# Differential attention: the low-half product of the scores on 64 of the 128 rows, in two row halves

## The chip, the cores and the metric

The program runs on one core of one Trainium2 chip. The metric is device microseconds of one execution; it was run three times, and the median is quoted. One further execution was recorded by the profiler, and all rows below are of that one.

## The reference

Two layers of a hybrid backbone over 128 context tokens and 1024 latent tokens. The change lies in the differential attention of the odd layer (4 heads; per head two softmaxes `p` = 0, 1 with 64 dimensions each; 1152 keys: 128 cached context keys and 1024 own ones):

```
s = einsum('bhqpd,bhkpd->bhpqk', qi, keys) * DH_C ** -0.5
p = softmax(s, axis=-1)
w = p[:, :, 0] - lam * p[:, :, 1]
o = einsum('bhqk,bhkv->bhqv', w, vals)
```

The context tokens have an attention of their own over 128 keys, through the same helper functions.

## The kernel before

Products that need more than the multiplier's one-pass precision are made from high and low halves: a value x is split into hi (rounded) and lo = x - hi, both of type fp32r, and `mm3` (lines 205 to 207) adds hi·hi, lo·hi and hi·lo in PSUM. The general matrix products of the projections and the feed-forward parts go through it.

`attention` (line 1300 on) does the 1024 latent queries of four heads, in 32 steps `n`, eight tiles of 128 queries per head. For each head `load` (L1348 to L1363) brings from DRAM: `q`, on 128 partitions the 64 dimensions of the queries' high halves and below them the 64 of the low halves, for both softmaxes; `kh`, the keys' high halves, twice (partitions 0 to 63 and 64 to 127); `kl`, their low halves, also twice; and the values `v`. One matmul of `q` with `kh` thus contracts 128 rows and gives (q hi + q lo)·k hi, and one with `kl` gives (q hi + q lo)·k lo.

- `tails` (L1308): for two tiles and both softmaxes, four products of 128 queries with the last 128 keys in one PSUM bank, each `kh` then `kl`; one copy to SBUF (`xt`, ScalarE) and one maximum for all four (`xm`, L1318, VectorE).
- `weights` (L1321): for each softmax the scores of the first 1024 keys (`s`, two PSUM banks, two such tiles in all), per bank `kh` then `kl` (L1328), four matmuls of 128 by 512; then `softmax` (L1199): maximum over `s` on VectorE (L1205), combined with `xm` (L1207), the exponentials on ScalarE (L1214) with their sums, the sums added (L1216), the reciprocal (L1217).
- `weigh` (L1220) calls `softmax` twice and merges the two results (L1227, L1228).
- `values` (L1334): nine transposes of the merged weights in three PSUM banks of tag `b` (L1340), three copies to `w` (ScalarE, VectorE, ScalarE), and nine full-precision matmuls with `v` (L1344), which the trace records as 18.

TensorE is filled between these steps by the output projection of finished parts (`mix_group`, tiles `w` and `ad`, L205 to L207) and, at the beginning, by the modulation of the second layer (`ada`, L384), whose weights `adaw` are 1 MB per transfer.

The order of the instructions on each engine is set when the program is built: a scheduler places each instruction by its priority and by a simulated timeline (`urgent` raises the priority), and the engines then run that fixed order. TensorE, VectorE and ScalarE each work through their own list, and an instruction that waits holds what stands behind it. All of the loads named here are issued by SyncE.

Of the kernel before, what the change touches and what calls it, by code (L numbers as in the profile page):

```python
# [10 lines left out]
F32 = mybir.dt.float32  # L11
F32R = mybir.dt.float32r
U32 = mybir.dt.uint32
AF = mybir.ActivationFunctionType
ALU = mybir.AluOpType
# [3 lines left out]
P = 128  # L19
# [3 lines left out]
NTOK = 1152  # L23
# [171 lines left out]
class Kern:  # L195
# [1000 lines left out]
                self.attention_prompt(al, "p", (2 * hb, 2 * hb + 1))  # L1196


    def softmax(self, pool, parts, tag, r, bufs=2):  # L1199

        nc = self.nc
        n = sum(x.shape[1] for x, _ in parts)
        p = pool.tile([P, n], F32, tag=f"{tag}{n}", name=tag, bufs=bufs)
        mx = pool.tile([P, 1], F32, tag=f"smx{n}", name="smx")
        nc.vector.tensor_reduce(mx, parts[0][0], AX.X, ALU.max)  # L1205
        if len(parts) == 2:
            nc.vector.tensor_scalar(mx, mx, parts[1][1], -0.125, ALU.max, ALU.mult)  # L1207
        else:
            nc.vector.tensor_scalar(mx, mx, -0.125, None, ALU.mult)
        sm = pool.tile([P, 2], F32, tag=f"ssm{n}", name="ssm", bufs=4)  # L1210
        o = n
        for i, (x, _) in reversed(list(enumerate(parts))):
            o -= x.shape[1]
            nc.scalar.activation(p[:, o:o + x.shape[1]], x, AF.Exp, scale=0.125, bias=mx, accum_out=sm[:, i:i + 1])  # L1214
        if len(parts) == 2:
            nc.vector.tensor_tensor(sm[:, 0:1], sm[:, 0:1], sm[:, 1:2], ALU.add)  # L1216
        nc.vector.reciprocal(r, sm[:, 0:1])  # L1217
        return p, sm[:, 0:1]

    def weigh(self, pool, scores, r1, tag, bufs=2):  # L1220

        nc = self.nc
        r2 = pool.tile([P, 1], F32, tag="r2" + tag, name="r2")
        with self.urgent():
            p1, s1 = self.softmax(pool, scores(0), "p0", r1, bufs)
            p2, _ = self.softmax(pool, scores(1), "p1", r2)
        nc.vector.tensor_scalar(r2, r2, self.nlam, s1, ALU.mult, ALU.mult)  # L1227
        nc.vector.scalar_tensor_tensor(p1, p2, r2, p1, ALU.mult, ALU.add)  # L1228
        return p1

    def attn_tokens(self, ps, r1, ob, ss, junk):
# [71 lines left out]
    def attention(self, hp, pool, last):  # L1303


        nc = self.nc

        def tails(t, q, kh, kl):  # L1308

            ps = self.bank("b")  # L1310
            for j in range(4):
                for x, kx in enumerate((kh, kl)):
                    nc.tensor.matmul(ps[:, 128 * j:128 * j + 128], q[:, j % 2, 128 * (t + j // 2):128 * (t + j // 2) + 128],
                                     kx[:, j % 2, 1024:1152], start=(x == 0), stop=(x == 1))
            xt = pool.tile([P, 4, P], F32, tag="xt", name="xt", bufs=3)
            self.copy(nc.scalar, xt, ps.rearrange("p (j k) -> p j k", j=4))
            xm = pool.tile([P, 4], F32, tag="xm", name="xm", bufs=3)
            nc.vector.tensor_reduce(xm, xt, AX.X, ALU.max)  # L1318
            return [(xt[:, j], xm[:, j:j + 1]) for j in range(4)]

        def weights(t, q, kh, kl, tail):  # L1321
            r1 = pool.tile([P, 1], F32, tag="r1", name="r1", bufs=4)

            def scores(p):
                s = self.ps["s"].tile([P, 1024], F32, tag="s", name="s", bufs=self.psb["s"] // 2)
                for k0 in (0, 512):
                    for x, kx in enumerate((kh, kl)):
                        nc.tensor.matmul(s[:, k0:k0 + 512], q[:, p, 128 * t:128 * t + 128], kx[:, p, k0:k0 + 512],  # L1328
                                         start=(x == 0), stop=(x == 1))
                return [(s, None), tail[2 * (t % 2) + p]]  # L1330

            return self.weigh(pool, scores, r1, "s", 3), r1

        def values(p1, r1, v, ob, ss):  # L1334
            w = pool.tile([P, NT, P], F32, tag="w", name="w", bufs=2)
            for g in range(3):
                pt = self.bank("b", 384)
                for j in range(3):
                    c = 3 * g + j
                    nc.tensor.transpose(pt[:, 128 * j:128 * j + 128], p1[:, 128 * c:128 * c + 128], self.ident)  # L1340
                self.copy((nc.scalar, nc.vector, nc.scalar)[g], w[:, 3 * g:3 * g + 3], pt.rearrange("p (c t) -> p c t", c=3))
            po = self.bank("b", P)
            for c in range(NT):
                nc.tensor.matmul(po, w[:, c], v[:, c], start=(c == 0), stop=(c == NT - 1))  # L1344
            junk = pool.tile([P, P], F32, tag="junk", name="junk")
            self.attn_tokens(po, r1, ob, ss, junk)

        def load(h, after=None):  # L1348

            q = hp.tile([P, 2, 1024], F32R, tag="q", name="q")  # L1350
            kh = hp.tile([P, 2, NTOK], F32R, tag="kh", name="kh")
            kl = hp.tile([P, 2, NTOK], F32R, tag="kl", name="kl")
            v = hp.tile([P, NT, P], F32, tag="v", name="v")
            if after is not None:
                for x in (q, kh, kl, v):
                    self.copy(nc.vector, x[:, 1, 0:1], after)
            nc.sync.dma_start(q[:].bitcast(F32), self.qT[2 * h:2 * h + 2].rearrange("j p t -> p j t"))
            for x in range(2):
                nc.sync.dma_start(kh[64 * x:64 * x + 64].bitcast(F32), self.kT[2 * h:2 * h + 2, 0:64].rearrange("j p t -> p j t"))
                nc.sync.dma_start(kl[64 * x:64 * x + 64].bitcast(F32), self.kT[2 * h:2 * h + 2, 64:128].rearrange("j p t -> p j t"))  # L1360
            nc.sync.dma_start(v[:, 0], self.A["cache_diff_v"][0, 0, h])
            nc.sync.dma_start(v[:, 1:], self.vals[1:, :, 128 * h:128 * h + 128].rearrange("i p d -> p i d"))
            return (q, kh, kl), v  # L1363

        loaded, tail, before, done = {}, {}, None, None
        for n in range(33):
            h, t = n // 8, n % 8
            if n == 0:
                loaded[0] = load(0)
                tail[0] = tails(0, *loaded[0][0])  # L1370
            if n < 32:
                if t == 0:
                    ob = pool.tile([P, 8, P], F32, tag="ob", name="ob")
                    ss = pool.tile([P, 8], F32, tag="ss", name="ss")
                w = weights(t, *loaded[h][0], tail[n // 2])
                now = w + (loaded[h][1], ob[:, t], ss[:, t:t + 1])
                if t == 2 and h < 3:
                    loaded[h + 1] = load(h + 1, w[1] if h == 0 else None)
                if t % 2 and n < 31:
                    tail[n // 2 + 1] = tails((t + 1) % 8, *loaded[(n + 1) // 8][0])  # L1380
            if n:
                values(*before)
                if n in (8, 16, 24, 28, 32):
                    a = slice(0, 8) if n < 28 else slice(0, 4) if n < 32 else slice(4, 8)
                    done = n, old[0][:, a], old[2], 128 + 128 * a.start, last if n > 24 else None
                    self.attn_norm(pool, done[1], old[1][:, a])
            if done and n in (done[0] + 2, 32):
                self.attn_out("b", *done[1:])
                done = None
            before, old = now, (ob, ss, h)  # L1390
            yield
# [243 lines left out]
```

## Time and profile before

| what | us |
|---|---|
| median of 3 runs | 3513.89 (3511.16 to 3518.72) |
| profiled execution, its own time | 3512.49 |
| span of that execution | 3510.7 |
| TensorE busy in the span | 3329.9 (95%) |
| VectorE, ScalarE, GpSimd busy | 1880.7, 1349.7, 870.9 |

The share of an engine is an average over stages with different limits, and a matmul's busy time contains the tail in which its results drain. What a change in one stage is worth is read from that stage, which here lies between 2272 us (first `tails`) and 2605 us (last `values`) of the span.

### The profile page before, as it was taken

Reading aid. Unit: us, or ns where it says so; the run is one execution under the profiler, and the core shown is the slowest. Engines: PE = TensorE matmul, PEld = TensorE weight load, DVE = VectorE, ACT = ScalarE, POOL = GpSimd, SP = SyncE. Lnnn points to the kernel's source line nnn. Section 1 sums busy time; section 2 is a strip of 40 time slices with the busy share of each in tenths; the row PEclk is TensorE's granted clock in tenths of the full one; section 3 lists DMA queues with packets and bytes.
Section 4 is the critical chain, followed back from the end, with each engine's and each line's share of the span. In section 5 each row is a group of like instructions: output and inputs, shape, how many; then the busy total and the mean of one; then the engine's idle time right before and its main releaser. Section 6 shows DMA issues by size and latency. Waiting matters only on the chain.

```text
span 3510.7 us, 55883 instructions
## 1 busy us (share of the span) xinstructions
PE 3329.9 (95%) x23022; PEld 3023.3 (86%) x23022; DVE 1880.7 (54%) x3342; ACT 1349.7 (38%) x2412; POOL 870.9 (25%) x596
## 2 busy tenths in 40 slices
PE   5999999888899999999999999989988999999998
PEld 2999999756689999999988999857767999999997
DVE  5658987488652333333372446458886233343334
ACT  5334333454543222232264434356565322232223
POOL 2432230001442222232240003301124222232214
PEclk7999999999899999999999999999998999999999
DMA  6445434483511110111143342583123111111104
GB/s 218 137 148 151 119 103 137 162 293 121 169 60 49 37 42 28 52 49 43 36 148 114 114 141 75 159 265 97 39 97 103 43 43 30 43 54 43 38 29 138
DMA packets 272700, 348.08 MB, mean 99 GB/s; under 512 B 14354, under 2 KB 231597, under 8 KB 266302
## 3 DMA queue, kind: packets, MB, share of 16 engines
q1 hardware_dynamic: 269294, 334.82, 30.2%
q0 software_dynamic: 3152, 9.70, 0.9%
q8 instruction: 181, 2.97, 0.4%
q14 instruction: 73, 0.60, 0.1%
HBM read 266.58 MB, written 77.89 MB: 98 GB/s over the span
## 4 chain that ended last, share of the span: by engine, by line
PE 78%; DVE 8%; DMA 6%; ACT 3%; issue 2%; POOL 2%; SPq 1%; POOLq 0%; DVEq 0%; ACTq 0%
PE g L206 9%; PE g L207 8%; PE g L205 8%; PE a L206 7%; PE a L205 7%; PE a L207 7%; PE d L205 5%; PE d L206 5%; PE d L207 5%; DMA adaw<-in_ada_w 2%; PE b L1344 1%; DVE f L442 1%; PE s L1328 1%; DVE acc L1002 1%; PE w L205 1%
## 5 line engine op out<-in xcount | busy, mean ns | idle before, releaser
L206 PE MATMUL g<-hTl,whi 128*128 128x388 f32 (+2 forms) x1728 | 591.1, 342 | 2.2 <-POOL hTl L218 2.2
L205 PE MATMUL g<-hTh,whi 128*128 128x388 f32 (+2 forms) x1728 | 590.6, 342 | 2.3 <-ACT hTh L445 2.3
L207 PE MATMUL g<-hTh,wlo 128*128 128x388 f32 (+2 forms) x1728 | 589.3, 342 | 0.0
L205 PE MATMUL a<-hTh,whi 128*128 128x388 f32 (+2 forms) x1248 | 427.3, 342 | 2.5 <-ACT hTh L445 1.4
L206 PE MATMUL a<-hTl,whi 128*128 128x388 f32 (+2 forms) x1248 | 427.3, 342 | 2.4 <-POOL hTl L218 2.3
L207 PE MATMUL a<-hTh,wlo 128*128 128x388 f32 (+2 forms) x1248 | 423.8, 342 | 0.1
L1002 DVE TENSOR_TENSOR acc<-d,acc 128x512 f32<-128x512 f32 x288 | 197.6, 688 | 334.0 <-PE d L207 332.7
L1104 POOL TENSOR_TENSOR ta<-ta,tg 128x386 f32<-128x386 f32 x132 | 135.7, 1028 | 916.6 <-ACT tg L1103 882.4
L205 PEld LDWEIGHTS g<-hTh,whi 128*128 128x128 f32 x1728 | 328.2, 190 | 6.7 <-ACT hTh L445 2.9
L206 PEld LDWEIGHTS g<-hTl,whi 128*128 128x128 f32 x1728 | 327.7, 190 | 6.6 <-POOL hTl L218 2.9
L207 PEld LDWEIGHTS g<-hTh,wlo 128*128 128x128 f32 x1728 | 327.5, 190 | 2.0
L205 PE MATMUL d<-dh,ah 128*128 128x512 f32 x792 | 312.7, 395 | 1.3 <-DVE acc L1002 1.3
L206 PE MATMUL d<-dl,ah 128*128 128x512 f32 x792 | 312.1, 394 | 0.0
L207 PE MATMUL d<-dh,al 128*128 128x512 f32 x792 | 312.0, 394 | 0.0
L476 ACT ACTIVATE tg<-g,cols,cols 128x386 f32<-128x386 f32 x132 | 88.8, 673 | 499.3 <-PE g L207 499.0
L218 POOL TENSOR_TENSOR wlo<-wraw,whi 128x1024 fp32r<-128x1024 f32 x90 | 217.0, 2411 | 167.7 <-ACT whi L211 167.7
L218 POOL TENSOR_TENSOR dl<-draw,dh 128x1024 fp32r<-128x1024 f32 x60 | 147.1, 2452 | 403.0 <-ACT dh L211 331.5
L205 PEld LDWEIGHTS a<-hTh,whi 128*128 128x128 f32 x1248 | 236.7, 190 | 11.3 <-issue 2.2
L206 PEld LDWEIGHTS a<-hTl,whi 128*128 128x128 f32 x1248 | 236.7, 190 | 9.6 <-POOL hTl L218 3.5
L477 DVE SCALAR_TENSOR_TENSOR tg<-g,cols,tg 128x386 f32<-128x386 f32 x132 | 81.8, 620 | 296.0 <-ACT tg L476 296.0
L207 PEld LDWEIGHTS a<-hTh,wlo 128*128 128x128 f32 x1248 | 236.6, 190 | 4.4 <-issue 1.6
L211 ACT ACTIVATE whi<-wraw 128x1024 fp32r<-128x1024 f32 x145 | 152.5, 1053 | 181.1 <-DMA wraw<-in_ffn_up 67.9
(429 smaller groups left out, 7031.8 us busy)
## 6 DMA issues: line engine op xcount, KB each, us to landing
adaw<-in_ada_w SPq DMA_DIRECT2D x48, 1024.0 KB
wraw<-in_ffn_up SPq DMA_DIRECT2D x88, 512.0 KB
draw<-in_ffn_down SPq DMA_DIRECT2D x44, 512.0 KB
wraw<-in_w_in_even SPq DMA_DIRECT2D x32, 512.0 KB
wraw<-in_w_in_odd SPq DMA_DIRECT2D x24, 512.0 KB
hgT<-po SPq DMA_DIRECT2D x16, 576.0 KB
ymid<-acc SPq DMA_DIRECT2D x18, 512.0 KB
y<-ymid SPq DMA_DIRECT2D x18, 512.0 KB
```

Source lines behind the costliest of these rows:

```text
L205: mm(out, lh, rh, start=start, stop=False)
L206: mm(out, lh, rl, start=False, stop=False)
L207: mm(out, ll, rh, start=False, stop=stop)
L211: eng.activation(out, in_, AF.Copy)
L218: eng.tensor_tensor(out, a, b, ALU.subtract)
L442: nc.vector.tensor_scalar(f[:, j], pt[:, 128 * j:128 * j + 128], mod[:, 1, g, k:k + 1], mod[:, 0, g, k:k + 1], ALU.mult, ALU.add)
L476: nc.scalar.activation(out, ps[:, 1:1 + n], AF.Identity, scale=w[1], bias=b)
L477: nc.vector.scalar_tensor_tensor(out, ps[:, 0:n], w[0], out, ALU.mult, ALU.add)
L1002: nc.vector.tensor_tensor(acc[:, i, s], ps, acc[:, i, s], ALU.add)
L1104: nc.gpsimd.tensor_tensor(ta, ta, tg, ALU.mult)
L1328: nc.tensor.matmul(s[:, k0:k0 + 512], q[:, p, 128 * t:128 * t + 128], kx[:, p, k0:k0 + 512], start=(x == 0), stop=(x == 1))
L1344: nc.tensor.matmul(po, w[:, c], v[:, c], start=(c == 0), stop=(c == NT - 1))
```

## The change

- `load` brings `kl` once: the low halves of the first softmax's keys on partitions 0 to 63, those of the second on 64 to 127. The second softmax's `q` is stored with its halves exchanged, so that the high halves of its queries lie on partitions 64 to 127. `q` takes three transfers in place of one.
- The product with `kl` contracts 64 rows, q hi with k lo, on partitions 0 to 63 for the first softmax and 64 to 127 for the second. The term q lo·k lo is no longer computed.
- `weights` writes the products of both softmaxes ahead of the first `softmax`: four with `kh`, then four with `kl`, alternating between the two.
- `tails` uses one bank and one copy per softmax, where it used one for both.
- The sums and reciprocals of both softmaxes are made by one addition and one reciprocal; one copy (`r1`) is added.
- The second of the three copies of `values` moves from VectorE to ScalarE.

```diff
     def weigh(self, pool, scores, r1, tag, bufs=2):
...
+        sm = pool.tile([P, 2, 2], F32, tag="ssm" + tag, name="ssm", bufs=4)
+        r = pool.tile([P, 2], F32, tag="r2" + tag, name="r2")
         with self.urgent():
-            p1, s1 = self.softmax(pool, scores(0), "p0", r1, bufs)
-            p2, _ = self.softmax(pool, scores(1), "p1", r2)
-        nc.vector.tensor_scalar(r2, r2, self.nlam, s1, ALU.mult, ALU.mult)
-        nc.vector.scalar_tensor_tensor(p1, p2, r2, p1, ALU.mult, ALU.add)
+            first = scores(0)
+            p1 = self.softmax(pool, first, "p0", [sm[:, i, 0:1] for i in range(2)], bufs)
+            p2 = self.softmax(pool, scores(1), "p1", [sm[:, i, 1:2] for i in range(2)])
+            if len(first) == 2:
+                nc.vector.tensor_tensor(sm[:, 0], sm[:, 0], sm[:, 1], ALU.add)
+            nc.vector.reciprocal(r, sm[:, 0])
+        nc.vector.tensor_copy(r1, r[:, 0:1])
+        nc.vector.tensor_scalar(r[:, 1:2], r[:, 1:2], self.nlam, sm[:, 0, 0:1], ALU.mult, ALU.mult)
+        nc.vector.scalar_tensor_tensor(p1, p2, r[:, 1:2], p1, ALU.mult, ALU.add)
...
         def tails(t, q, kh, kl):
-            ps = self.bank("b")
-            for j in range(4):
-                for x, kx in enumerate((kh, kl)):
-                    nc.tensor.matmul(ps[:, 128 * j:128 * j + 128], q[:, j % 2, 128 * (t + j // 2):128 * (t + j // 2) + 128],
-                                     kx[:, j % 2, 1024:1152], start=(x == 0), stop=(x == 1))
             xt = pool.tile([P, 4, P], F32, tag="xt", name="xt", bufs=3)
-            self.copy(nc.scalar, xt, ps.rearrange("p (j k) -> p j k", j=4))
+            for p in range(2):
+                ps = self.bank("b", 256)
+                x = slice(64 * p, 64 * p + 64)
+                for j in range(2):
+                    o, z = ps[:, 128 * j:128 * j + 128], slice(128 * (t + j), 128 * (t + j) + 128)
+                    nc.tensor.matmul(o, q[:, p, z], kh[:, p, 1024:1152], start=True, stop=False)
+                    nc.tensor.matmul(o, q[x, p, z], kl[x, 1024:1152], start=False, stop=True)
+                self.copy(nc.scalar, xt[:, p::2], ps.rearrange("p (j k) -> p j k", j=2))
...
         def weights(t, q, kh, kl, tail):
+            s = [self.ps["s"].tile([P, 1024], F32, tag="s", name="s", bufs=self.psb["s"] // 2) for p in range(2)]
+            z = slice(128 * t, 128 * t + 128)
+            with self.urgent():
+                for p in range(2):
+                    for k0 in (0, 512):
+                        nc.tensor.matmul(s[p][:, k0:k0 + 512], q[:, p, z], kh[:, p, k0:k0 + 512], start=True, stop=False)
+                for k0 in (0, 512):
+                    for p in range(2):
+                        x = slice(64 * p, 64 * p + 64)
+                        nc.tensor.matmul(s[p][:, k0:k0 + 512], q[x, p, z], kl[x, k0:k0 + 512], start=False, stop=True)
+
             def scores(p):
-                s = self.ps["s"].tile([P, 1024], F32, tag="s", name="s", bufs=self.psb["s"] // 2)
-                for k0 in (0, 512):
-                    for x, kx in enumerate((kh, kl)):
-                        nc.tensor.matmul(s[:, k0:k0 + 512], q[:, p, 128 * t:128 * t + 128], kx[:, p, k0:k0 + 512],
-                                         start=(x == 0), stop=(x == 1))
-                return [(s, None), tail[2 * (t % 2) + p]]
+                return [(s[p], None), tail[2 * (t % 2) + p]]
...
-                self.copy((nc.scalar, nc.vector, nc.scalar)[g], w[:, 3 * g:3 * g + 3], pt.rearrange("p (c t) -> p c t", c=3))
+                self.copy(nc.scalar, w[:, 3 * g:3 * g + 3], pt.rearrange("p (c t) -> p c t", c=3))
...
-            kl = hp.tile([P, 2, NTOK], F32R, tag="kl", name="kl")
+            kl = hp.tile([P, NTOK], F32R, tag="kl", name="kl")
...
-            nc.sync.dma_start(q[:].bitcast(F32), self.qT[2 * h:2 * h + 2].rearrange("j p t -> p j t"))
+            nc.sync.dma_start(q[:, 0].bitcast(F32), self.qT[2 * h])
+            for x in range(2):
+                nc.sync.dma_start(q[64 * x:64 * x + 64, 1].bitcast(F32), self.qT[2 * h + 1, 64 - 64 * x:128 - 64 * x])
             for x in range(2):
                 nc.sync.dma_start(kh[64 * x:64 * x + 64].bitcast(F32), self.kT[2 * h:2 * h + 2, 0:64].rearrange("j p t -> p j t"))
-                nc.sync.dma_start(kl[64 * x:64 * x + 64].bitcast(F32), self.kT[2 * h:2 * h + 2, 64:128].rearrange("j p t -> p j t"))
+                nc.sync.dma_start(kl[64 * x:64 * x + 64].bitcast(F32), self.kT[2 * h + x, 64:128])
```

The change moves instructions. In the kernel before, TensorE's list for one tile in the middle of the stage reads as follows (`s_23574` and `s_23588` are the scores of the two softmaxes of one tile, `w_...` are tiles of the output projection, `x3` stands for three in a row):

```order
L1328 MATMUL s_23574<-kh_23108,q_23107 128x512
L1328 MATMUL s_23574<-kl_23109,q_23107 128x512
L1328 MATMUL s_23574<-kh_23108,q_23107 128x512
L1328 MATMUL s_23574<-kl_23109,q_23107 128x512
L205 MATMUL w_25115<-dh_24991,mxh_24995 128x512
L206 MATMUL w_25115<-dl_24992,mxh_24995 128x512
L207 MATMUL w_25115<-dh_24991,mxl_24996 128x512
L205 MATMUL w_25115<-dh_25002,mxh_25006 128x512
L206 MATMUL w_25115<-dl_25003,mxh_25006 128x512
L207 MATMUL w_25115<-dh_25002,mxl_25007 128x512
L1328 MATMUL s_23588<-kh_23108,q_23107 128x512
L1328 MATMUL s_23588<-kl_23109,q_23107 128x512
```

Here `kh` and `kl` alternate per bank, all on 128 rows, and six matmuls of the projection lie between the two softmaxes.

In the changed kernel (L1333 is the product with `kh`, L1337 the one with `kl` on 64 rows) such a tile reads:

```order
L1333 MATMUL s_23153<-kh_22542,q_22541 128x512 x2
L1337 MATMUL s_23153<-kl_22543,q_22541 128x512 x2
L205 MATMUL w_25007<-dh_24963,mxh_24967 128x512
L206 MATMUL w_25007<-dl_24964,mxh_24967 128x512
L207 MATMUL w_25007<-dh_24963,mxl_24968 128x512
L205 MATMUL w_25007<-dh_24974,mxh_24978 128x512
L206 MATMUL w_25007<-dl_24975,mxh_24978 128x512
L207 MATMUL w_25007<-dh_24974,mxl_24979 128x512
L1333 MATMUL s_23154<-kh_22542,q_22541 128x512 x2
L1337 MATMUL s_23154<-kl_22543,q_22541 128x512 x2
L1350 MATMUL b_23121<-ident_76,p0_23006 128x128 x3
```

The written order of four and four stands only in the first tile (L1333 four times, then L1337 four times, its writes alternating between `s_22404` and `s_22405`). In the other 31 tiles the scheduler has parted the two softmaxes: two products with `kh`, two on 64 rows into the same `s` tile, so of the same row half, and then something else.

For the last keys TensorE's list in the changed kernel has (L1318 the product with `kh`, L1319 the one on 64 rows):

```order
L1318 MATMUL b_23030<-kh_22542,q_22541 128x128
L1319 MATMUL b_23030<-kl_22543,q_22541 128x128
L1318 MATMUL b_23030<-kh_22542,q_22541 128x128
L1319 MATMUL b_23030<-kl_22543,q_22541 128x128
L1350 MATMUL b_23039<-ident_76,p0_22942 128x128 x3
```

Here each product on 64 rows stands alone between two on 128 rows, as all 64 of them do. Counted over the list, the matmuls on 64 rows stand in 127 uninterrupted runs: 64 runs of one (L1319), 62 of two and one of four (L1337). Of these, 29 (16 and 13) stand ahead of the last `ada` matmul (L384), and 98 behind it.

## Rows read from the trace of the kernel before

**Rows 1.** The page: busy time of each engine.

```profile
PE 3329.9 (95%) x23022; PEld 3023.3 (86%) x23022; DVE 1880.7 (54%) x3342; ACT 1349.7 (38%) x2412; POOL 870.9 (25%) x596
```

**Rows 2.** Busy time by stretch; columns as in its first row.

```profile
core 0: us, PE busy (x) PEld busy (x) DVE busy (x) ACT busy (x) POOL busy (x), PEclk, DMA share, GB/s
2272.00:2335.00 63.00, 49.43 (x262) 31.69 (x261) 35.22 (x79) 33.44 (x76) 13.52 (x12) 0.88 0.92 295
2335.00:2605.00 270.00, 248.93 (x1527) 206.18 (x1526) 204.78 (x404) 159.79 (x391) 27.67 (x12) 0.98 0.28 82
```

**Rows 3.** Chain that ended last, 2272 to 2335 us: start, us, what.

```profile
2275.25 10.98 DMA adaw<-in_ada_w
...
2314.03 18.54 DMA adaw<-in_ada_w
```

**Rows 4.** The same chain, 2500 to 2530 us.

```profile
by line: PE s L1328 19.1%; PE b L1344 16.4%; PE w L207 9.4%; PE w L205 9.4%; PE b L1340 8.7%; PE w L206 8.5%; PE ad L207 8.5%; PE ad L206 7.7%; PE ad L205 7.6%; PE b L1313 5.6%
...
2502.14 0.93 PE s L1328 x4
...
2512.50 2.01 PE b L1344 x18
...
2524.90 0.84 PE b L1313 x8
```

**Rows 5.** The same chain, 2335 to 2605 us: its longest pieces on VectorE and DMA.

```profile
2475.92 2.41 DVE ssm L1216
2490.05 2.64 DMA mixT<-ob
2492.74 3.60 DMA mxl<-mixT
```

**Rows 6.** TensorE's timeline around a context-attention product on 64 rows (L1287).

```profile
2268.77 0.28 PE L205 MATMUL a<-whi,hTh 128*128 128x256 f32 x1
2268.88 0.28 PE L206 MATMUL a<-wlo,hTh 128*128 128x256 f32 x1
2269.00 0.28 PE L207 MATMUL a<-whi,hTl 128*128 128x256 f32 x1
2269.21 0.48 PE L1287 MATMUL p<-pqk 64*128 64x128 f32 x2
2269.63 0.39 PE L205 MATMUL a<-whi,hTh 128*128 128x256 f32 x1
2269.85 0.28 PE L206 MATMUL a<-wlo,hTh 128*128 128x256 f32 x1
```

**Rows 7.** TensorE's timeline in the linear-attention scan, L586 and L587 on 64 rows.

```profile
2214.28 0.49 PE L583 MATMUL c<-v,att 128*128 128x128 f32 x2
2214.70 0.49 PE L586 MATMUL c<-sf,x 64*128 64x128 f32 x2
2215.02 0.38 PE L587 MATMUL c<-sb,x 64*128 64x128 f32 x2
2215.34 0.49 PE L583 MATMUL c<-v,att 128*128 128x128 f32 x2
```

**Rows 8.** The weight loads of the same stretch.

```profile
2214.70 0.29 PEld L586 LDWEIGHTS c<-sf,x 64*128 64x128 f32 x2
2214.91 0.30 PEld L587 LDWEIGHTS c<-sb,x 64*128 64x128 f32 x2
```

**Rows 9.** Timelines of L502: both row halves alternating (first row), one head on 128 rows.

```profile
2020.37 0.81 PE L502 MATMUL c<-x 64*64 64x64 f32 x40
...
871.47 1.27 PE L502 MATMUL c<-x 128*64 128x64 f32 x36 [0.38 <-DVE x L541]
```

**Rows 10.** Groups by line, 2335 to 2605 us: busy us, mean ns, idle before.

```profile
L211 ACT ACTIVATE w<-b 128x384 f32<-128x384 f32 x59 | 28.7, 486 | 40.3 <-PE b L1340 40.3
L215 DVE COPY w<-b 128x384 f32<-128x384 f32 x29 | 15.9, 549 | 3.1 <-PE b L1340 3.1
L1216 DVE TENSOR_TENSOR ssm<-ssm 128x1 f32<-128x1 f32 x54 | 14.6, 270 | 12.5 <-ACT p L1214 12.1
L1217 DVE RECIPROCAL r<-ssm 128x1 f32<-128x1 f32 x54 | 8.5, 160 | 1.2
L211 ACT ACTIVATE xt<-b 128x512 f32<-128x512 f32 x13 | 7.7, 593 | 11.7 <-PE b L1313 11.5
```

**Rows 11.** Waits, 2272 to 2605 us: us in total, times, longest.

```profile
PEld b L1344 <- DVE w L215: 3.9, 7, 1.1
PEld b L1344 <- ACT w L211: 3.3, 4, 0.8
```

**Rows 12.** DMA issues, 2272 to 2335 us: KB each.

```profile
kl<-kT SPq DMA_DIRECT2D x2, 576.0 KB
```

**Rows 13.** SyncE's timeline, 2240 to 2400 us.

```profile
2310.18 0.38 SPq L1357 DMA_DIRECT2D q<-qT x1
```

More of the change, by code (lines that the diff above doesn't have):

```diff
@@ L1196, in odd_qkv, with softmax @@
                 self.attention_prompt(al, "p", (2 * hb, 2 * hb + 1))
-    def softmax(self, pool, parts, tag, r, bufs=2):
+    def softmax(self, pool, parts, tag, sm, bufs=2):
         nc = self.nc
@@ L1213, in softmax @@
             o -= x.shape[1]
[L1214 to L1218, printed above, removed]
+            nc.scalar.activation(p[:, o:o + x.shape[1]], x, AF.Exp, scale=0.125, bias=mx, accum_out=sm[i])
+        return p
     def weigh(self, pool, scores, r1, tag, bufs=2):
         nc = self.nc
-        r2 = pool.tile([P, 1], F32, tag="r2" + tag, name="r2")
+        sm = pool.tile([P, 2, 2], F32, tag="ssm" + tag, name="ssm", bufs=4)
+        r = pool.tile([P, 2], F32, tag="r2" + tag, name="r2")
         with self.urgent():
-            p1, s1 = self.softmax(pool, scores(0), "p0", r1, bufs)
-            p2, _ = self.softmax(pool, scores(1), "p1", r2)
-        nc.vector.tensor_scalar(r2, r2, self.nlam, s1, ALU.mult, ALU.mult)
-        nc.vector.scalar_tensor_tensor(p1, p2, r2, p1, ALU.mult, ALU.add)
+            first = scores(0)
[7 more added lines that the diff above has]
+        nc.vector.scalar_tensor_tensor(p1, p2, r[:, 1:2], p1, ALU.mult, ALU.add)
         return p1
@@ L1351, in load @@
             kh = hp.tile([P, 2, NTOK], F32R, tag="kh", name="kh")
-            kl = hp.tile([P, 2, NTOK], F32R, tag="kl", name="kl")
+            kl = hp.tile([P, NTOK], F32R, tag="kl", name="kl")
             v = hp.tile([P, NT, P], F32, tag="v", name="v")
             if after is not None:
-                for x in (q, kh, kl, v):
-                    self.copy(nc.vector, x[:, 1, 0:1], after)
-            nc.sync.dma_start(q[:].bitcast(F32), self.qT[2 * h:2 * h + 2].rearrange("j p t -> p j t"))
+                for x in (q[:, 1, 0:1], kh[:, 1, 0:1], kl[:, 0:1], v[:, 1, 0:1]):
+                    self.copy(nc.vector, x, after)
+            nc.sync.dma_start(q[:, 0].bitcast(F32), self.qT[2 * h])
+            for x in range(2):
+                nc.sync.dma_start(q[64 * x:64 * x + 64, 1].bitcast(F32), self.qT[2 * h + 1, 64 - 64 * x:128 - 64 * x])
             for x in range(2):
                 nc.sync.dma_start(kh[64 * x:64 * x + 64].bitcast(F32), self.kT[2 * h:2 * h + 2, 0:64].rearrange("j p t -> p j t"))
-                nc.sync.dma_start(kl[64 * x:64 * x + 64].bitcast(F32), self.kT[2 * h:2 * h + 2, 64:128].rearrange("j p t -> p j t"))
+                nc.sync.dma_start(kl[64 * x:64 * x + 64].bitcast(F32), self.kT[2 * h + x, 64:128])
             nc.sync.dma_start(v[:, 0], self.A["cache_diff_v"][0, 0, h])
```

1 line of the change is left out of this document (removed).

## The prediction

> **What bounds the kernel now.** The page is read first: TensorE is busy for 95% of the span, no other engine for more than 54% [rows 1]. That is an average, so the stage is cut out next. The change touches almost only the latent attention, which runs from 2272 to 2605 us. In the busy time by stretch it falls into two parts [rows 2]. Up to 2335 us the DMA engines are busy 92% of the time and TensorE idles 63.0 - 49.4 = 13.6 us; the chain that ended last says why, since its long pieces there are transfers of `adaw` [rows 3]. From 2335 us on TensorE is busy 248.9 of 270 us, idle 21.1, and VectorE 204.8: one engine bounds, a second stands close. Where in that part TensorE is really the bound is read from the chain again: between 2500 and 2530 us every piece of it lies on TensorE [rows 4], so there a nanosecond more of TensorE is a nanosecond more of time; elsewhere it runs through VectorE's wait for a sum (2.4 us) or through a store and reload of `mixT` (2.6 and 3.6 us) [rows 5], and there TensorE has air.
>
> The same chain gives the prices of work at full flow: four score matmuls of 128 by 512 take 0.93 us, 0.23 each; 18 of `values` take 2.01 and eight of `tails` 0.84, 0.11 each [rows 4].
>
> **The products on 64 rows.** Their number does not change: per tile four of 128 by 512 and, per pair of tiles, four of 128 by 128 with `kl`, as before. A product on half of the rows is not shorter by itself: the 64-row matmuls of the scan follow each other as closely as others (next paragraph). So alone they save nothing. They would save something if two on different row halves ran at once, and the trace shows that this chip does that: with both row halves alternating 40 matmuls of L502 take 0.81 us, where on 128 rows 36 take 1.27 [rows 9]. But TensorE's list of the changed kernel alternates in one tile of 32 (one saving of 2 x 0.23 us, left out); in the other 31 the two 64-row products of a run go to the same half.
>
> **What entering and leaving 64 rows costs.** Two places show it. Around L1287 [rows 6], from the last full matmul ahead (L207, 2269.00) to the second one behind (L206, 2269.85) pass 0.85 us. In that time stand L207 and L205 (0.115 each, by the starts of the rows above) and two 64-row ones (0.11): 0.45 us of work. The run costs **0.40 us** extra, the two gaps (enter, leave) together. In the scan [rows 7] one round from L583 to the next L583 takes 2215.34 - 2214.28 = 1.06 us for six matmuls of 0.11 (0.67): **0.39** extra, for one run of four. So the price belongs to the run, not to the matmul. The Trainium skill has a rule for this, in "TensorEngine Tiling (Array Packing)", section Tiling Modes: changing the tiling mode, and not merely the tile, drains TensorE. It gives no price; it speaks against this change, and the trace agrees with it by the 0.39 us.
>
> Those two rows are of fp32 products; a 64-row product of type fp32r, as here, is nowhere in the trace. Bounds: 0 (if fp32r needed no drain) and 0.40. I take 0.39, since what surrounds L1287 is fp32r work and pays it on both sides.
>
> In TensorE's list there are 127 runs. Of them 29 stand ahead of the last `ada` matmul, in the part that waits for `adaw`: 29 x 0.39 = 11.3 us lie in 13.6 us of idle time, and I cost them at nothing. Were that cover gone, they would cost their 11.3. The other 98 stand in the part bound by TensorE: 98 x 0.39 = **38.2 us**.
>
> **What idle time takes back.** The 21.1 us of idle time behind 2335 us can swallow some of it, where a run's gaps fall into a wait that is there anyway. Bounds 0 and 21.1. Half of the chain pieces that are off TensorE are in the softmax's own loop (scores, maximum, exponentials), which a gap in the scores lengthens too, so I take a third: **-7 us**.
>
> **Transfers.** The `kl` transfers shrink from 576 KB to half. Two of them fall into the stretch in which DMA bounds [rows 12]: 0.59 MB less at 295 GB/s [rows 2] is **-2 us**; for the other heads the transfers are hidden (DMA is busy 28%). `q` needs two more issues per head on SyncE's queue, 0.38 us each [rows 13], ahead of `kh`, `kl` and `v`; behind them stands `adaw`. For the one head in that stretch 0.8 us, inside the bounds of this term (-2 to +1).
>
> **VectorE and ScalarE.** Per tile VectorE loses a copy to `w` (0.549), one addition (0.270) and one reciprocal (0.160) and gains a copy of one column (no row; bounded by 0 and 0.270, taken like the reciprocal as 0.160): 32 x 0.82 = 26 us off an engine that is busy 205 of 270 [rows 2, 10]. TensorE's own waits for that copy are 3.9 us [rows 11]. ScalarE gains 32 x 0.486 = 15.6 us, and per pair of tiles a second copy of `xt` (between 0 and 0.593, so up to 9.5 us) [rows 10]; it goes from 160 to at most 185 of 270 us and is no bound, but its list now has three copies in a row where two engines shared them, and TensorE's wait for ScalarE's copies, 3.3 us [rows 11], may double. The merged sum makes VectorE wait for the second exponentials instead of both; behind it stand the next maxima. Net, between -6 and +3: **-3 us**. Two banks instead of one in `tails` also ask for one more turn of the two `b` banks per pair of tiles; that lies within these bounds.
>
> **Sum.** 38.2 - 7 - 2 - 3 = 26 us, against the profiled execution's 3512.5 us: 3538.7, rounded to **3539**. That execution lies 1.4 us below the median of 3513.9, within the spread of the three.
>
> **The rivals.**
>
> *No drain between fp32r products.* If entering 64 rows cost nothing for this type, only the savings would be left: 2 us of transfers, and of VectorE's 26 us as much as TensorE's waits give back, at most half of its idle time, 10 us: 3512.5 - 12 = **3500**. Place: the gap between L1333 and L1337. It decides at a price per run of 0.12 us, where 98 runs cost what the other terms (7 + 2 + 3) take back. For it: no such product is in the trace. Against it: fp32r neighbours pay on both sides of L1287 [rows 6]. Chance 0.10.
>
> *The gaps vanish in waits.* If all idle time of the second part took them up and VectorE gave its 6: 38.2 - 21.1 - 2 - 6 = 9 us, **3521**, and a little less with the full DMA gain, hence no measurable change. For it: the softmax's chain is long. Against it: stretches without any idle piece in the chain [rows 4]. Chance 0.10.
>
> *The second product of a run waits for its weights.* If two 64-row products of the same half could not overlap the load of one with the run of the other, each of the 62 pairs would lose up to one load, 0.19 us (0.30 for two loads that start 0.11 apart [rows 8]): 12 us on top, **3551**. The trace speaks against it: L587's two loads overlap, and the round of six pays only its two gaps [rows 7, 8]. The Trainium skill states it as a rule, in "TensorE: Matmul & The Clock Gate", Part 3: a weight load overlaps a running matmul only where the row group differs. By that rule the pairs would pay; by the rows they do not. Chance 0.04.
>
> *The change does what its words say.* If each tile ran its four 64-row products alternating, it would save 2 x 0.23 us and one run: 32 x 0.46 + 31 x 0.39 = 27 us less than forecast, **3512**. The list of instructions is fixed when the program is built and shows it once. Chance 0.01.
>
> **How the numbers follow.** The forecast has the remaining 0.75. About 0.2% (7 us) is what a measurement of this kernel can tell from no change. The forecast's own bounds are 38.2 - 21 - 2 - 6 = 9 us and, with nothing taken back, half of the 29 hidden runs showing (6 us) and VectorE and ScalarE at +3, 47 us: 3522 to 3560. The second rival is taken in half, the third fully, which leaves out the first and the ends: 3512 to 3562. Faster 0.10 (first rival), same 0.10 (second and fourth), slower 0.80.
>
> **What would show it.** In the changed kernel's timeline a gap of about 0.2 us ahead of each L1337 and L1319 run and behind it; TensorE's share of the chain in the second part higher, VectorE's lower; VectorE's busy time some 26 us less; the last `values` some 26 us later and everything behind it shifted by as much. I would be wrong if the scores' four matmuls, now in two runs, still followed each other at 0.23 us across the change of rows, or if idle time on TensorE in the second part fell by more than the third I took.

## The result and the profile after

The changed kernel takes 3542.65 us (median of 4 runs, 3537.03 to 3543.24), the kernel before, run beside it, 3516.3 (4 runs, 3511.16 to 3523.0): a ratio of 1.0068, with an interval from 1.0049 to 1.0086. It is slower by 26 us where 3539 us in all, 26 more, were forecast. The profiled execution took 3542.44 us, its span is 3540.3.

The page of the changed kernel, busy time of each engine, as [rows 1] of before:

```profile
PE 3369.7 (95%) x23022; PEld 3022.0 (85%) x23022; DVE 1867.1 (53%) x3278; ACT 1364.6 (39%) x2460; POOL 864.3 (24%) x596
```

TensorE runs the same 23022 matmuls and is busy 39.8 us longer. To see where, I cut out the part that TensorE bounds: from the end of the last `ada` matmul (L384) to the end of the last matmul of `values`. It is called the late part from here on. In the kernel before it goes from 2367.0 to 2601.3 us, in the changed one from 2365.8 to 2629.0. Busy time in it, of before and then of after (columns as in [rows 2]):

```profile
2367.00:2601.30 234.30, 215.04 (x1322) 183.39 (x1321) 187.07 (x367) 141.19 (x347) 27.43 (x10) 0.99 0.23 65
```

```profile
2365.80:2629.00 263.20, 253.51 (x1350) 188.27 (x1347) 175.99 (x328) 157.73 (x397) 26.43 (x10) 0.97 0.20 56
```

The late part is 28.9 us longer, the whole span 29.6: ahead of it the change gains 1.2 us, behind it 909.4 us pass before and 911.3 after. TensorE's idle time falls from 19.3 to 9.7 us, and its busy time grows by 38.5.

The place is seen in TensorE's timeline of the changed kernel, one tile whose two softmaxes follow each other:

```profile
2427.78 0.40 PE L207 MATMUL w<-dh,mxl 128*128 128x512 f32 x1
2428.01 0.63 PE L1333 MATMUL s<-kh,q 128*128 128x512 f32 x2
2428.57 0.73 PE L1337 MATMUL s<-kl,q 64*128 64x512 f32 x2
2429.23 0.73 PE L1333 MATMUL s<-kh,q 128*128 128x512 f32 x2
2429.89 0.73 PE L1337 MATMUL s<-kl,q 64*128 64x512 f32 x2
2430.55 0.51 PE L205 MATMUL w<-dh,mxh 128*128 128x512 f32 x1
2430.90 0.40 PE L206 MATMUL w<-dl,mxh 128*128 128x512 f32 x1
```

Two matmuls of this size take 0.46 us from start to start at 0.23 each. Here the first pair takes 0.56 to the next start, each of the other three 0.66, and the L205 behind the last run 0.35. From 2428.01 to 2430.90 pass 2.89 us for nine matmuls, 2.07 at 0.23: two runs cost 0.82, 0.41 each.

What stands ahead of the gap, by the waits of line L1337 over the whole span (us, times):

```profile
  issue: 23.5, 63
```

The weight loads of 63 runs, every one that L1337 has, stood idle for 0.37 us each, and no other engine and no transfer released them: the gap is TensorE's own. That idle time lies ahead of a run and is not a run's price, which happens to be as large: on 128 rows in one experiment below (e1) the loads stand idle for 0.04 us at the same place.

### The profile page after: what moved, and what is told of

Same layout as the page of the kernel before. It is cut to its first block, busy times and chain, and to the rows that moved or that the text cites. A ratio compares the mean times of both kernels' runs of the same rounds, so it can differ in the third digit from the quotient of the medians.

```text
span 3540.3 us, 55915 instructions
## 1 busy us (share of the span) xinstructions
PE 3369.7 (95%) x23022; PEld 3022.0 (85%) x23022; DVE 1867.1 (53%) x3278; ACT 1364.6 (39%) x2460; POOL 864.3 (24%) x596
## 3 DMA queue, kind: packets, MB, share of 16 engines
HBM read 264.22 MB, written 77.89 MB: 97 GB/s over the span
## 4 chain that ended last, share of the span: by engine, by line
PE 80%; DVE 7%; DMA 5%; ACT 3%; issue 2%; POOL 1%; SPq 0%; POOLq 0%; ACTq 0%; DVEq 0%
PE g L206 9%; PE g L207 9%; PE g L205 9%; PE a L205 7%; PE a L206 7%; PE a L207 7%; PE d L205 5%; PE d L206 5%; PE d L207 5%; PE b L1354 2%; DMA adaw<-in_ada_w 2%; DVE f L442 1%; PE s L1337 1%; PE w L205 1%; DVE acc L1002 1%
## 5 line engine op out<-in xcount | busy, mean ns | idle before, releaser
L206 PE MATMUL g<-hTl,whi 128*128 128x388 f32 (+2 forms) x1728 | 591.2, 342 | 2.2 <-POOL hTl L218 2.2
L205 PE MATMUL g<-hTh,whi 128*128 128x388 f32 (+2 forms) x1728 | 590.6, 342 | 2.3 <-ACT hTh L445 2.3
L205 PE MATMUL a<-hTh,whi 128*128 128x388 f32 (+2 forms) x1248 | 427.3, 342 | 2.8 <-ACT hTh L445 1.4
L206 PE MATMUL a<-hTl,whi 128*128 128x388 f32 (+2 forms) x1248 | 427.4, 342 | 0.6 <-POOL hTl L218 0.6
L205 PEld LDWEIGHTS g<-hTh,whi 128*128 128x128 f32 x1728 | 328.3, 190 | 6.7 <-ACT hTh L445 2.9
L206 PEld LDWEIGHTS g<-hTl,whi 128*128 128x128 f32 x1728 | 327.9, 190 | 6.6 <-POOL hTl L218 2.9
L205 PE MATMUL d<-dh,ah 128*128 128x512 f32 x792 | 312.7, 395 | 1.1 <-DVE acc L1002 1.1
L206 PE MATMUL d<-dl,ah 128*128 128x512 f32 x792 | 312.2, 394 | 0.0
L205 PEld LDWEIGHTS a<-hTh,whi 128*128 128x128 f32 x1248 | 236.8, 190 | 12.0 <-issue 2.9
L206 PEld LDWEIGHTS a<-hTl,whi 128*128 128x128 f32 x1248 | 236.8, 190 | 7.1 <-issue 1.1
```

The lines of the kernel that those rows point to most:

```text
L205: mm(out, lh, rh, start=start, stop=False)
L206: mm(out, lh, rl, start=False, stop=False)
```

## The experiments

All kernels start from the changed one. Ratios are to the kernel before, run on the same chip beside them.

| kernel | median us (lowest to highest, runs) | ratio, interval |
|---|---|---|
| changed | 3542.65 (3537.03 to 3543.24, 4) | 1.0068, 1.0049 to 1.0086 |
| e1, no 64-row product | 3517.42 (3508.18 to 3526.91, 10) | 1.0001, 0.9987 to 1.0016 |
| e2, scores alone on 64 rows | 3541.22 (3539.78 to 3546.95, 4) | 1.0078, 1.0057 to 1.0099 |
| e3, last keys alone on 64 rows | 3533.31 (3526.78 to 3539.34, 6) | 1.0048, 1.0031 to 1.0065 |
| e8, scores in twice as many runs | 3573.62 (3562.6 to 3576.72, 4) | 1.0162, 1.0131 to 1.0192 |
| e5, as e1, second copy on VectorE | 3521.86 (3516.6 to 3530.31, 10) | 1.0015, 1.0004 to 1.0026 |
| e6, as e1, last keys in one bank | 3514.22 (3509.95 to 3524.41, 10) | 0.9991, 0.9978 to 1.0004 |
| e7, as e5 and e6 together | 3520.42 (3511.11 to 3524.81, 12) | 1.0004, 0.9993 to 1.0015 |
| e2b, as e2, smaller pools | 3573.59 (1 run) | |
| e4, as e2b, key halves on the two row halves | 3538.12 (1 run) | |

**e1: the low product back on 128 rows.** The loads of `kl` and `q` go back with it (not shown here); the merged sums, the second bank of `tails`, the third copy on ScalarE and the scores written ahead are kept.

```diff
-                    nc.tensor.matmul(o, q[x, p, z], kl[x, 1024:1152], start=False, stop=True)
+                    nc.tensor.matmul(o, q[:, p, z], kl[:, p, 1024:1152], start=False, stop=True)
...
-                        nc.tensor.matmul(s[p][:, k0:k0 + 512], q[x, p, z], kl[x, k0:k0 + 512], start=False, stop=True)
+                        nc.tensor.matmul(s[p][:, k0:k0 + 512], q[:, p, z], kl[:, p, k0:k0 + 512], start=False, stop=True)
```

> The changed kernel with the product with the keys' low halves on all 128 rows again (kl and q loaded as in the kernel before); merged sums, the tails' two banks and the third copy on ScalarE stay. Theory A (each run of matmuls on 64 rows costs TensorE 0.37 us, of which about 0.32 shows for the 98 late ones): the 31 us go, so 3511 us, about 5 below the kernel before. Rival B (the loss comes from the other parts: three copies in a row on ScalarE, a second bank per tails): 3535 to 3543.

Measured: 3517.42 us, not to be told from before, where 5 us below it were expected. The 64-row products, with the loads that belong to them, are the whole loss, 25.2 us by the medians (3542.65 - 3517.42); the edits that e1 keeps are worth nothing together that can be measured. TensorE's timeline of e1 shows the same stretch of a tile without gaps (L1336 is the product with `kl`):

```profile
2416.07 0.62 PE L1333 MATMUL s<-kh,q 128*128 128x512 f32 x2
2416.53 0.62 PE L1336 MATMUL s<-kl,q 128*128 128x512 f32 x2
2416.99 0.62 PE L1333 MATMUL s<-kh,q 128*128 128x512 f32 x2
2417.44 0.61 PE L1336 MATMUL s<-kl,q 128*128 128x512 f32 x2
2417.89 1.50 PE L1353 MATMUL b<-v,w 128*128 128x128 f32 x12
```

Eight matmuls take 1.82 us. With e1 beside the changed kernel the price of a run can be read by its neighbours: the time from the last 128-row matmul ahead of the low products to the second one behind them, median in the late part, in ns.

| run, followed by | runs | e1 | changed | extra |
|---|---|---|---|---|
| scores, projection (L205, L206) | 11 | 929 | 1324 | 395 |
| scores, `values` | 11 | 804 | 1199 | 395 |
| scores, transposes | 18 | 808 | 1151 | 343 |
| scores, other four kinds | 10 | | | 344 to 490 |
| last keys, the next of their kind | 28 | 366 | 745 | 379 |
| last keys, transposes | 12 | 356 | 677 | 321 |
| last keys, others | 8 | 506 | 844 | 338 |

Summed over the 98 runs this is 36.2 us, 0.37 each.

The late part of e1, as above:

```profile
2365.70:2593.30 227.60, 213.35 (x1313) 179.41 (x1314) 165.18 (x312) 152.08 (x381) 27.60 (x10) 1.00 0.22 61
```

It starts at the same time as the changed kernel's and is 35.6 us shorter, but the granted clock was 1.00 in it against 0.97. This one execution lies 9.2 us below e1's median (3508.2 to 3517.4). Length times granted clock, which is fair as far as TensorE bounds the part and good to a microsecond or so by the rounding of the clock, gives 227.6 and 255.3 us: 27.7 at equal clock, near the 25.2 of the medians.

The two parts don't hold the same work, though. Behind the last `ada` matmul TensorE's list has 1345 matmuls in the changed kernel and 1312 in e1 (1319 before): one `values`, four transposes and eleven products of the scores more. `values` (18 matmuls each) by stretch, e1 and then the changed kernel (TensorE, its weight loads):

```profile
2365.70:2593.30 227.60, 61.58 (x486) 59.38 (x486) 0.00 (x0) 1.00 0.22 61
```

```profile
2365.80:2629.00 263.20, 65.64 (x504) 61.25 (x504) 0.00 (x0) 0.97 0.20 56
```

At 0.11 and 0.23 us each [rows 4] these 33 matmuls are 5.0 us of work, which e1 does earlier. So of the 27.7 us some 22.7 are left for the 98 runs, and of their 36.2 us waits took back 13.5; by the medians it is 36.2 + 5.0 - 25.2 = 16.

**e2 and e3: the scores alone, and the last keys alone, on 64 rows.** e2 loads the low halves of the last 128 keys into a small tile of its own, `kt`, on 128 partitions, for the last keys' products; e3 takes `kl` as in e1, with the scores' line of e1's diff, and leaves the last keys on 64 rows. Of e2:

```diff
-                    nc.tensor.matmul(o, q[x, p, z], kl[x, 1024:1152], start=False, stop=True)
+                    nc.tensor.matmul(o, q[:, p, z], kt[:, p], start=False, stop=True)
```

> The changed kernel with the tails' product on 128 rows again (their part of kl is loaded once more, 64 KB per transfer); the scores' product stays on 64 rows, 63 runs, 48 of them late. Theory A: 48 x 0.32 = 15 us above the version with all on 128 rows, so 3526 us. Rival C (nearly all of it comes from the tails, where each matmul stands alone between two changes of rows): 3513. Rival B: 3535 to 3543.

> The changed kernel with the scores' product on 128 rows again (kl loaded on all rows); the tails' product stays on 64 rows, 64 runs, 48 late. Theory A: 48 x 0.32 = 15 us above the version with all on 128 rows, so 3526 us. Rival C: 3540. Rival B: 3535 to 3543.

Late parts of e2 and of e3:

```profile
2380.10:2625.30 245.20, 230.91 (x1320) 174.08 (x1318) 168.78 (x318) 151.91 (x381) 27.50 (x10) 0.99 0.20 55
```

```profile
2369.80:2614.80 245.00, 232.90 (x1346) 194.02 (x1347) 172.22 (x328) 158.29 (x397) 26.43 (x10) 0.98 0.24 65
```

Over e1's 227.6 they are 17.6 and 17.4 us longer, 15.1 and 12.5 at equal clock (length times clock), for 48 late runs each; the two add to 27.6, where the changed kernel has 27.7. How these differences are shared says little of the price: e3's late part, like the changed kernel's, holds 33 matmuls (5.0 us) that e1 does earlier, e2's only four (0.8 us). The price is read from the gaps, by the measure of the table: a late run of two takes 1152 ns ahead of transposes and 1199 ahead of `values` in e2, a run of one 676 ahead of transposes and 745 ahead of the next of its kind in e3, as in the changed kernel. Summed over the 48 runs this is 0.39 us each for the scores and 0.36 for the last keys, although a product of the last keys has a quarter of the columns: the price belongs to the run. The times don't add, and both missed the expected 3526: e3 is 16 us above e1, and e2, with 24, fell into the range of rival B. In e2 the last `ada` matmul ends 14 us later. Its chain says why:

```profile
2319.24 9.55 DMA kl<-kT
2328.86 9.47 DMA adaw<-in_ada_w
```

In SyncE's list of the changed kernel six `adaw` transfers stand ahead of a head's loads, in that of e2 five, and the sixth behind them. SyncE's timelines, the changed kernel first, then e2:

```profile
2296.13 21.19 SPq L382 DMA_DIRECT2D adaw<-in_ada_w  x6
```

```profile
2297.59 19.76 SPq L382 DMA_DIRECT2D adaw<-in_ada_w  x5
...
2328.86 0.36 SPq L382 DMA_DIRECT2D adaw<-in_ada_w  x1
```

That was not expected; e2's late part answers the question, its total doesn't.

**e8: the scores' products in twice as many runs.** Per block of 512 keys `kh`, then `kl` on 64 rows, so each 64-row product stands alone; the same matmuls.

```diff
+                    x = slice(64 * p, 64 * p + 64)
                     for k0 in (0, 512):
                         nc.tensor.matmul(s[p][:, k0:k0 + 512], q[:, p, z], kh[:, p, k0:k0 + 512], start=True, stop=False)
-                for k0 in (0, 512):
-                    for p in range(2):
-                        x = slice(64 * p, 64 * p + 64)
                         nc.tensor.matmul(s[p][:, k0:k0 + 512], q[x, p, z], kl[x, k0:k0 + 512], start=False, stop=True)
```

> The changed kernel with the scores' products written per block of 512 keys, kh then kl, so that each matmul on 64 rows of the scores stands alone: the same matmuls, 128 runs in place of 63 for the scores, 100 late in place of 50. Theory A (the price belongs to the run): 50 x 0.32 to 0.37 = 16 to 19 us more than the changed kernel, 3559 to 3561 us. Rival D (the price belongs to the matmul on 64 rows, however they stand): no change, 3543.

Measured: 31 us above the changed kernel. The late part:

```profile
2374.90:2659.20 284.30, 275.68 (x1349) 196.88 (x1347) 174.34 (x328) 158.71 (x397) 26.39 (x10) 0.96 0.18 52
```

It is 21.1 us longer than the changed kernel's, 17.6 at equal clock, for 50 more late runs: 0.35 each. This is the cleanest of the differences, since behind the last `ada` matmul both lists hold the same 1345 matmuls. What the expectation missed is the early part: the last `ada` matmul ends 9.1 us later. 15 runs more stand there, 44 in all, and 44 x 0.37 = 16 us are more than the 13.6 us of idle time in [rows 2]; that this is the cause fits, but no run shows it alone.

**e4 and e2b: two row halves at once.** In e4 the low product of the first 512 keys lies on partitions 0 to 63 and that of the second on 64 to 127, for each softmax, so the two products of a run are of different halves and no scheduler can part them. It needs a tile `qh` with the queries' high halves on both; to make room the pools of `p` and `xt` have one buffer less. e2b is e2 with those smaller pools, as its yardstick. First the edit of the pools, then that of e4's scores:

```diff
-            xt = pool.tile([P, 4, P], F32, tag="xt", name="xt", bufs=3)
+            xt = pool.tile([P, 4, P], F32, tag="xt", name="xt", bufs=2)
...
-            return self.weigh(pool, scores, r1, "s", 3), r1
+            return self.weigh(pool, scores, r1, "s", 2), r1
```

```diff
-                for k0 in (0, 512):
-                    for p in range(2):
-                        x = slice(64 * p, 64 * p + 64)
-                        nc.tensor.matmul(s[p][:, k0:k0 + 512], q[x, p, z], kl[x, k0:k0 + 512], start=False, stop=True)
+                for p in range(2):
+                    for i in range(2):
+                        x = slice(64 * i, 64 * i + 64)
+                        nc.tensor.matmul(s[p][:, 512 * i:512 * i + 512], qh[x, p, z], kl[x, p], start=False, stop=True)
```

> The version with the scores' product on 64 rows and the tails' on 128, with two buffers in place of three for the weights p0 and for xt: made only to stand beside the next one, which needs that memory. Read from the last ada matmul to the last matmul of values (late part): 245 us as with three buffers, if the buffers do not bind; 49 late runs of two matmuls on the same row half, 1.32 us each from the last full matmul ahead to the second projection matmul behind.

> The same, but the two matmuls on 64 rows of a run are the two blocks of 512 keys of one softmax, the first on partitions 0 to 63, the second on 64 to 127 (the queries' high halves lie on both, one more tile and two more transfers per head), so that they alternate whatever the scheduler does. Theory A (row halves of type fp32r run at once, the run keeps its price of 0.39 us): the run 0.23 us shorter, 1.09 us by the same measure; late part 42 to 49 x 0.23 = 10 to 11 us shorter than the version beside it, still some 7 us longer than with all on 128 rows (0.39 - 0.23 = 0.16 per run). Rival E (fp32r halves do not overlap at the full clock): 1.32 us and no change.

TensorE's timeline of e4:

```profile
2448.16 0.71 PE L1333 MATMUL s<-kh,q 128*128 128x512 f32 x2
2448.80 0.50 PE L1337 MATMUL s<-kl,qh 64*128 64x512 f32 x2
2449.23 0.50 PE L205 MATMUL w<-dh,mxh 128*128 128x512 f32 x1
2449.57 0.40 PE L206 MATMUL w<-dl,mxh 128*128 128x512 f32 x1
```

From the first L1337 to L205 pass 0.43 us, in the changed kernel 0.66: 0.23 less, one whole product. Two fp32r products on the two halves do run at once. By the measure of the table above such a run takes 1097 ns ahead of the projection, against 1324 in the changed kernel, and still 168 more than the 929 of four products on 128 rows. So even the alternation that the change is named for doesn't pay in runs of this length. In total e4 is 35 us below e2b. Its 64 runs give at most 64 x 0.23 = 15 us of that (22 of them stand ahead of the last `ada` matmul). The rest is not the runs': e2b's late part had the lowest granted clock of all (first row, e4's in the second),

```profile
2366.10:2657.50 291.40, 264.24 (x1360) 197.01 (x1358) 175.72 (x331) 155.99 (x394) 25.84 (x10) 0.91 0.18 51
```

```profile
2420.30:2627.30 207.00, 196.89 (x1189) 153.78 (x1190) 153.05 (x291) 138.48 (x346) 25.84 (x10) 0.98 0.19 56
```

0.91 of 291.4 us, some 26 us of full speed lost, where e4's had 0.98. Nor can the late parts be set against each other, as was meant: e4's last `ada` matmul ends 54 us later, with more of the work ahead of it. Each of the two kernels ran once.

**e5, e6, e7: the other edits.** e5 is e1 with the second copy of `values` on VectorE again, e6 is e1 with the last keys in one bank with one copy, e7 is both, so that of the change only the merged sums and the scores written ahead remain. First e5's edit, then e6's:

```diff
-                self.copy(nc.scalar, w[:, 3 * g:3 * g + 3], pt.rearrange("p (c t) -> p c t", c=3))
+                self.copy((nc.scalar, nc.vector, nc.scalar)[g], w[:, 3 * g:3 * g + 3], pt.rearrange("p (c t) -> p c t", c=3))
```

```diff
+            ps = self.bank("b")
+            for j in range(4):
+                for x, kx in enumerate((kh, kl)):
+                    nc.tensor.matmul(ps[:, 128 * j:128 * j + 128], q[:, j % 2, 128 * (t + j // 2):128 * (t + j // 2) + 128],
+                                     kx[:, j % 2, 1024:1152], start=(x == 0), stop=(x == 1))
...
-                self.copy(nc.scalar, xt[:, p::2], ps.rearrange("p (j k) -> p j k", j=2))
+            self.copy(nc.scalar, xt, ps.rearrange("p (j k) -> p j k", j=4))
```

> All products on 128 rows, and the second of the three copies of values back on VectorE; merged sums and two banks stay. If moving the copy to ScalarE was a gain (VectorE relieved by 32 x 0.55 = 18 us): late part 228 to 232 us, 1 to 4 longer than with it on ScalarE, 3518 to 3521 us. Rival F (three copies in a row on ScalarE hold up values): 2 to 4 us shorter, 3513 to 3516.

> All products on 128 rows, and the tails in one bank with one copy as in the kernel before; merged sums and the third copy on ScalarE stay. If the second bank and copy cost something: late part 2 to 5 us shorter, 3512 to 3515 us. If they are hidden: 3517. Either way the lowest of the versions tried so far or level with it.

> The change's merged sums and reciprocals alone, with the scores of both softmaxes written ahead: all low products on 128 rows, last keys in one bank with one copy, second copy to w on VectorE as before. Theory A (the three other edits are worth what they gave one by one): e1 (3517.4) with the copy back on VectorE (+4.4, from e5) and one bank (-3.2, from e6): 3518 to 3519, ratio 1.000 to 1.001, not to be told from before; late part 240 to 250 us, since VectorE has the copy again. Rival B (the merged sums are the gain that the copy and the banks give back): an addition of 0.27 and a reciprocal of 0.16 less per tile on the softmax's chain, 32 times, up to 14 us less than before: 3503 to 3509, ratio 0.996 to 0.998. Rival C (merging makes the first softmax wait for the second one's exponentials, and this costs): 3524 or more, ratio over 1.002.

All lie within 0.2% of before, and their intervals overlap with e1's; only e5's leaves out 1. A gain of some 4 us from the copy on ScalarE and a loss of 3 from the second bank are what the medians suggest and the intervals don't show. The medians of e5 and e6 came out close to what was expected of a gain and of a loss, but the late parts did not (242.1 us in e5, where 228 to 232 were expected, and 233.1 in e6, where it was to be shorter than e1's 227.6), at granted clocks of 0.97 in both against 1.00. e7's ratio is what theory A expected; its late part is not (217.9 us where 240 to 250 were expected), since the last `ada` matmul ended 24 us later than in the changed kernel and work had moved ahead of it. None beats the kernel before measurably; the lowest is e6.

## Why the prediction was right

**The price of a run, 0.39 us: right, for fp32r too.** It was taken from fp32 rows [rows 6, 7]. Read by neighbours it is 0.32 to 0.40 for nearly all runs, 0.37 in the mean, so 98 late runs are worth 36.2 us in place of 38.2. The Trainium skill's rule, in "TensorEngine Tiling (Array Packing)", section Tiling Modes, that a changed tiling mode drains TensorE, agrees with the trace: L1337's 63 gaps of 0.37 us.

**The 29 early runs at nothing: right for the end of the early part, not for the work in it.** The last `ada` matmul ends no later, at 2365.8 us after 2367.0 before and 2365.7 in e1. But up to there the changed kernel does 5.0 us less of the attention's work than e1. TensorE's idle time from 2272 us to that point is 8.5 us, in e1 11.5. So of the 10.7 us that 29 runs are worth at 0.37, some 3 fit into idle time, 5.0 into the room of work that now runs later, and some 2 into the clock's difference (0.93 of 94 us against 0.91); this is a count over two single executions. The order is set when the program is built, and e3, with 16 early runs, has the same 33 matmuls behind the last `ada` matmul; why the scheduler sets it so stays open.

**What idle time takes back, 7 us: right in kind, half of what was measured.** It is 13.5 us by the late parts at equal clock and 16 by the medians, inside the forecast's bounds of 0 and 21.1. The raw difference of the late parts, 35.6, would have said next to nothing: the two executions differ in clock and in work. Of TensorE's recorded idle time only 14.3 - 9.7 = 4.6 us went between e1 and the changed kernel. A record lasts 0.39 us where the next start follows after 0.23, so a short wait does not appear as idle time; where the rest was taken back is not shown. The prediction would call itself wrong if idle time in the second part fell by more than 7 us: from 2335 us to just behind the last `values` it fell from 21.07 to 13.34, by 7.7, and in the late part by 9.6. That sign came, if barely, and it points at the size of this term.

**Transfers -2, VectorE and ScalarE -3: not seen.** The traffic fell as worked out, from 266.58 to 264.22 MB read, four times 0.59. VectorE's edited groups fell nearly as worked out. In the groups by line of before they are the copies to `w`, 17.6 us, 64 additions, 16.1, and 72 reciprocals, 11.5; after, over the whole span:

```profile
L1226 DVE TENSOR_TENSOR ssm<-ssm 128x2 f32<-128x2 f32 x32 | 10.4, 324 | 18.0 <-ACT p L1213 17.9
L1227 DVE RECIPROCAL r<-ssm 128x2 f32<-128x2 f32 x36 | 5.8, 162 | 3.7 <-ACT p L1213 3.0
L1228 DVE COPY r<-r 128x1 f32<-128x1 f32 x36 | 5.2, 146 | 0.4
```

That is 45.2 - 21.4 = 23.8 us less, where 26 were forecast: the merged addition takes 324 ns, not the 270 of a single one. VectorE's busy time as a whole fell by only 13.6, since groups that the change doesn't touch came out longer. In time the edits of VectorE and ScalarE are worth 0.0 us, with an interval from -5 to +6 (e1): the -3 lies in it, and is neither shown nor refuted. The smaller transfers were never run alone. The last `ada` matmul ends at 2365.8 us with them and at 2365.7 without (e1), so in these two executions no gain of 2 us shows where it was to come.

**The sum.** Forecast 38.2 + 0 - 7 - 5 = 26 us; by the experiments 36.2 + 5.0 - 16 + 0 = 25, and 26 by the medians of before and after. The late runs were priced 2 us too high, the early part moved 5 us of work into the late one where nothing was forecast, the take-back was 9 too small, and a gain of 5 did not show. Mechanism and price of a run were right; that the total met the measured time to a microsecond is luck, since these misses cancel.

**The rivals.** *No drain* falls by the timeline. *The gaps vanish in waits* falls by e1: 16 of the 36.2 us did at most, and 25 showed. *The second product waits for its weights* falls by the runs of one size: from the start of a run of the scores to the second transpose behind it pass 0.82 us with two products (changed kernel) and 0.59 with one (e8), medians in the late part; so the second product costs its own 0.23 and not a load's 0.19 more. (Its recorded start lies 0.34 us behind the first one's, but the run as a whole is longer by 0.23 only.) The weight loads of the changed kernel's tile above, of which the second row is a run's two loads on the same row half:

```profile
2427.78 0.42 PEld L1333 LDWEIGHTS s<-kh,q 128*128 128x128 f32 x2
2428.57 0.29 PEld L1337 LDWEIGHTS s<-kl,q 64*128 64x128 f32 x2 [0.37 <-issue]
```

Both loads are done 0.29 us after the run starts, while the first product's record lasts 0.49: the second load runs beside the first product. The Trainium skill's rule in "TensorE: Matmul & The Clock Gate", Part 3, that a load overlaps only a matmul of another row group, is not what these rows show. *What the words say* holds for one tile. The chain of the changed kernel has it, at a granted clock of 0.50:

```profile
2284.56 1.71 PE s L1333 x4
2286.28 1.15 PE s L1337 x4
```

The four alternating products take 1.15 us where the four on 128 rows take 1.71. In the other 31 the list has parted them. By the prices above, a run of four would save 2 x 0.23 us and cost 0.37, 0.09 in favour of it; that is an estimate, and no run shows such a run of four at the full clock.

## What to carry to other kernels

A product on half of the rows saved TensorE nothing by itself here and cost about 0.37 us each time the engine went to 64 rows and back, of which waits took back some four tenths where TensorE is the bound; count the runs in the scheduled list, not the matmuls in the code. Two halves at once save one product, here 0.23 us, so a run pays only if it holds enough alternating pairs to outweigh its own entry and exit, and only if no scheduler can part them. 24 us less on VectorE, which was not the bound, gave nothing that could be measured. And before two executions are compared by a part of them, count the matmuls in it: the part from one fixed instruction to another can hold different work.

## What was not expected

The granted clock made single profiled executions hard to compare: in the late part it was 1.00 in e1 and 0.91 in e2b. It is lost in stretches at 0.50 (1.2 GHz). In TensorE's timeline of e2b one begins behind a wait for the exponentials: the first pair below lasts 0.74 us, the second 1.22, where at full clock it lasts 0.73:

```profile
2507.37 0.74 PE L1333 MATMUL s<-kh,q 128*128 128x512 f32 x2 [1.27 <-ACT p L1213]
2508.04 1.22 PE L1337 MATMUL s<-kl,q 64*128 64x512 f32 x2
```

TensorE had idled 2.35 us of the ten from 2490 and 2.1 of the ten from 2500 us. Whether the changed kernel's 0.97 comes from the change or from that one execution stays open: each kernel was profiled once.

With one buffer less in each of two pools e2b's one execution took 32 us more than e2's median, with 27 us of TensorE's idle time in the late part against 14, and a granted clock of 0.91 against 0.99. Whether the buffers are the cause stays open: e4 has the same small pools and took 3538 us, less than e2.
